# The first SwiGLU half-step rebuilt in Strassen's form, and half of the modulation moved into the attention

## Chip, cores and metric

The kernel runs on one core of one Trainium2 chip. The metric is the device time of one launch in microseconds (us), the median of several runs of the same program. A profile is one further execution, recorded by the hardware profiler; its times are us from its first instruction unless marked ns.

## What is computed

One layer of a diffusion trunk: 512 latent and 128 context tokens (640 in all, the axis `T`), width 1024. Cut to what matters here:

```python
m = adaln(c)                                   # nine modulation vectors m[0..8], silu(c) @ w_ada + b_ada
hh = rmsnorm(x, g[0]) * (1 + m[1]) + m[0]
x = x + 0.5 * m[2] * (silu(hh @ w1) * (hh @ w3)) @ w2     # first half-step, 1024 -> 2816 -> 1024
hh = rmsnorm(x, g[1]) * (1 + m[4]) + m[3]
x = x + m[5] * token_mixer(hh)                            # differential attention (8 heads) and an mLSTM
hh = rmsnorm(x, g[2]) * (1 + m[7]) + m[6]
x = x + 0.5 * m[8] * (silu(hh @ w1b) * (hh @ w3b)) @ w2b  # second half-step
```

The results are the new x, new keys and values, and the final mLSTM states. Everything is float32.

## The kernel before

Features lie on the 128 partitions and tokens along the free axis; `HALF` is 320 tokens, `KT` = 8 tiles of the width, `FB` = 11 blocks of 256 hidden features. A float32 product is made of three matmuls of a rounded type: each operand is split into a high part (rounded by an ACT copy) and a low part (the difference, by one subtraction), and `mm3` adds high x high, high x low and low x high. One such product of a 128 x 128 tile of weights with 320 tokens is three matmuls of 320 columns.

TensorE's instructions stand in the order of the program (`keep_in_program_order`). The other engines' order is set when the program is built, by a planner that simulates durations and prefers, among what is ready, what comes first in the program. DMAs of weights and activations are issued by SP's queue. Weights arrive in two buffers, `raw`, of 1 MB, which all stages share.

**First half-step** (`first_half_step`, L233 on). The blocks `b` run in turn. A block has four up units (f, hf), each with 16 `mm3` on w1 and w3, then `glu` (silu on ACT, the product and the low part `gL` on DVE), and `down` adds the product of the block with w2 to x, tile by tile (16 tiles, 6 matmuls a block each), through `add_residual` on DVE. The weights' high parts are made by ACT and their low parts by POOL (`split_w`, the tiles `wL`, `w3L`). Beside it runs the modulation: `mod_tile` loads 1 MB of `w_ada_c` and makes two columns of it by two DVE products each, which add up along the row (`tensor_tensor_reduce`, with the tile `junk` as output); 28 such tiles give m2 to m8. m0 and m1 come at the very start through TensorE (`Modulate`, the tiles `mrow`, `ps_at`). In the last `down`, the first token half is finished before the second; `to_mixing` collects the squares, and the norm of the mixing for the first half (`norm2(0)`) runs beside the products of the second.

**Mixing.** Groups of the attention's projections come first (`tok_group`, with `norm2_second` inside). Then eight heads, each with five blocks of queries (`qi`): `scores` writes one PSUM tile `sc` that exists once; DVE takes its maximum (`mx`), ACT the exponentials, DVE the weighted difference (`p0`); one block later TensorE transposes it (`turn`, `ps_wT`) and multiplies it with the values (`values`, `ps_o`). In between, `fill.slot()` puts matmuls of other projections, whose weights are again split by ACT and POOL. The heads take from about 620 to 1140 us. Then come the mLSTM and the output projections.

**Second half-step** (from about 1500 us). It has Strassen's form in Winograd's variant: a product of 2 x 2 blocks takes seven block products in place of eight, with sums of the operands. Tokens (two halves) and features (two halves) form the 2 x 2 split; the seven operands are named A11, A12, S2, S1, S3, A22, S4. Block 0 is plain, two units at a time. Then `products` runs over granules: 20 for w1 and w3 of blocks 1 to 10 (`nk` = 4 tiles, 84 matmuls each) and 12 for w2. For each granule, `parts` and `sums` make the split weights and their sums (ACT and DVE alone); `done` receives the four results, adds the shared parts that ACT copied out of PSUM (the tiles `u`), and for w3 writes the gated products into `SO`. `store_g` forms the sums of a finished block in `SO`, makes the high part (ACT) and the low part (DVE) in `g`, and stores both to `g_dram`. For the way down, the blocks are taken in three groups of 4, 4 and 3, and the seven operands of a group come back from `g_dram` into the tiles S and hm:

```python
    GROUPS = ((0, 4), (4, 8), (8, FB))
    ...
    def operand(q, i):
        n = 7 * q + i
        at[q, i] = t = slots[n % 9]
        b0, b1 = GROUPS[q]
        nc.sync.dma_start(out=t[:, :, : b1 - b0].bitcast(F32), in_=g_dram[i, :, :, b0:b1, :])
```

Of the kernel before, what the change touches and what calls it, by code (L numbers as in the profile page):

```python
# [7 lines left out]
F32 = mybir.dt.float32  # L8
# [23 lines left out]
def tile_trunk(ctx: ExitStack, tc: tile.TileContext, a: dict):  # L32
# [52 lines left out]
    x_pool = right.enter_context(tc.tile_pool(name="x1", bufs=1, side="right"))  # L85
    x_all = x_pool.tile([128, KT, T], F32, name="x")
    x = [x_all[:, d, :] for d in range(KT)]
# [50 lines left out]
    def rstd_of(pool, ss, inv_n, shape, tag, bufs=1, ybufs=1):  # L138
        v = pool.tile(shape, F32, tag=tag + "v", name="rv", bufs=bufs)
        y = pool.tile(shape, F32, tag=tag + "y", name="ry", bufs=max(bufs, ybufs))  # L140
        t = pool.tile(shape, F32, tag=tag + "t", name="rt", bufs=bufs)
        ts(v, ss, inv_n, ALU.mult, EPS, ALU.add)
        act(t, v, AF.Ln)
        act(y, t, AF.Exp, scale=-0.5)
        newton_rsqrt(y, v, t)
        return y


    class Stats:


        def __init__(self, x, hf, tmp, eng=pool_e, tag="nsq"):
            self.x, self.hf, self.tmp, self.eng, self.tag = x, hf, tmp, eng, tag
            self.acc = tmp.tile([128, HALF], F32, tag="nacc", name="nacc", bufs=2)

        def add(self, d):
            xs = self.x[d][:, half(self.hf)]
            if d == 0:
                act(self.acc, xs, AF.Square)
                return  # L160
            sq = self.tmp.tile([128, HALF], F32, tag=self.tag, name="nsq", bufs=2)
            self.ins = act(sq, xs, AF.Square).ins  # L162
            if d < KT - 1:
                tt(self.eng, self.acc, self.acc, sq, ALU.add)
# [3 lines left out]
        def rstd(self, psum, ybufs=2):  # L168
# [3 lines left out]
            return rstd_of(self.tmp, ps[:, :HALF], 1.0 / D, [128, HALF], "nr", ybufs=ybufs)  # L172

    def norm_apply(x, n, m_shift, hf, d, rs, hH, hL, tmp):
        c0 = hf * HALF
        shift = m_of(m_shift)
        for s0, s1, j in SEGS[hf]:
            t = tmp.tile([128, HALF], F32, tag="nt", name="nt", bufs=2)
            tv = t[:, : s1 - s0]
            ins = stt(tv, x[d][:, s0:s1], scale[:, n, d, j : j + 1], rs[:, s0 - c0 : s1 - c0], ALU.mult, ALU.mult)  # L180
            sh = shift[:, d, j : j + 1]
            act(hH[:, d, s0:s1], tv, AF.Identity, bias=sh)
            if d % 2 == 0 or n == 0:
                stt(hL[:, d, s0:s1], tv, sh, hH[:, d, s0:s1].bitcast(F32), ALU.add, ALU.subtract)
            else:
                act(tv, tv, AF.Identity, bias=sh)
                tt(pool_e, hL[:, d, s0:s1], tv, hH[:, d, s0:s1].bitcast(F32), ALU.subtract)
        return ins.ins
# [13 lines left out]
    UNITS = [(f, hf) for hf in range(2) for f in range(2)]  # L202
# [3 lines left out]

    def up_group(psum, hh, W, units, g2, tmp, before, tag="g"):

        hH, hL = hh
        ps = [[acc_tile(psum) for _ in range(2)] for _ in units]  # L210
        for k in range(KT):
            before(k)
            for (f, hf), p in zip(units, ps):
                col = k * 256 + f * 128
                cs = half(hf)
                for i in range(2):
                    w = W[i]
                    mm3(p[i], w[0][:, col : col + 128], w[1][:, col : col + 128], hH[:, k, cs], hL[:, k, cs], k == 0, k == KT - 1)
        for (f, hf), p in zip(units, ps):
            glu(g2, f, hf, p, tmp, tag)  # L220

    def glu(g2, f, hf, ps, tmp, tag="g"):
        g = tmp.tile([128, HALF], F32, tag=tag, name="g", bufs=2)
        act(g, ps[0], AF.Silu)
        tt(vec, g, ps[1], g, ALU.mult)
        split_glu(g2, f, hf, g)

    def split_glu(g2, f, hf, g):
        gH, gL = g2
        cs = half(hf)  # L230
        act(gH[:, f, cs], g, AF.Copy)
        tt(vec, gL[:, f, cs], g, gH[:, f, cs].bitcast(F32), ALU.subtract)

    def down(psum, x, gate, blocks, final=None, at_once=1):

# [1532 lines left out]
```

## Time and profile before

| | |
|---|---|
| median of 3 runs | 1930.51 us (1930.28 to 1934.54) |
| the profiled execution | 1934.46 us, span 1932.7 us, mean granted clock 0.982 |
| TensorE busy | 1853.8 us, 96% of the span |
| DVE, ACT, POOL busy | 1280.2, 793.9, 491.5 us |

A matmul record is longer than its share of the engine, because matmuls are pipelined; the pitch is read from a stretch in which TensorE is never idle, by dividing it by the count. A row of the table of stretches gives the stretch, its length, the busy time and count (x) of each engine, the granted clock (1.00 is full), the DMA engines' share and GB/s. A row of groups gives busy time, the mean of one in ns, and the idle time before it with what ended it. In a row of the waits stand the total, the number and the longest.

### The profile page before, as it was taken

What the parts mean: (1) busy time and instruction counts of PE and PEld (TensorE: products, weight loads), DVE (VectorE), ACT (ScalarE), POOL (GpSimd) and SP (SyncE); (2) the same over time, 40 slices, a digit from 0 to 9 for tenths busy, and PEclk for the clock granted to TensorE, in tenths of its full rate; (3) what the DMA queues carried; (4) which work ended last, traced back from release to release, by engine and by line L of the source; (5) the groups of instructions that cost most, each with busy time, mean ns of one, the idle gap of its engine ahead of it and who ended that gap; (6) DMA issues with size and microseconds to landing.
All of it is one profiled execution on the core that took longest, in us unless ns stands there. A gap on an engine that the chain in (4) does not pass through costs nothing. (4 is left out here: it accounts for less than half of the span.)

```text
span 1932.7 us, 31309 instructions
## 1 busy us (share of the span) xinstructions
PE 1853.8 (96%) x12862; PEld 1813.1 (94%) x12862; DVE 1280.2 (66%) x2179; ACT 793.9 (41%) x1374; POOL 491.5 (25%) x183
## 2 busy tenths in 40 slices
PE   5999999999997999999999999999999999999899
PEld 4899999999997999999999998899999999999898
DVE  6898888864556565474575544654146888888776
ACT  4322111222454354454454435566234655554332
POOL 2134322343433223242232222224462000000000
PEclk8999999999998999999999999999999999999999
DMA  8344343442223112122122224445524255557864
GB/s 339 130 169 160 133 172 134 150 153 99 85 84 97 66 65 83 49 92 82 66 83 90 72 85 153 147 139 194 191 97 153 106 183 175 170 183 259 334 243 146
DMA packets 98896, 271.15 MB, mean 140 GB/s; under 512 B 7937, under 2 KB 66817, under 8 KB 81089
## 3 DMA queue, kind: packets, MB, share of 16 engines
q1 hardware_dynamic: 98752, 269.15, 39.7%
q8 instruction: 101, 1.65, 0.3%
q14 instruction: 43, 0.34, 0.1%
HBM read 216.97 MB, written 52.15 MB: 139 GB/s over the span
## 5 line engine op out<-in xcount | busy, mean ns | idle before, releaser
L39 POOL TENSOR_TENSOR wL<-raw,wH 128x2048 fp32r<-128x2048 f32 x67 | 312.3, 4663 | 756.5 <-ACT wH L118 741.7
L52 PE MATMUL ps_p<-hH,wH 128*128 128x320 f32 x864 | 275.2, 319 | 4.9 <-ACT aT L883 2.5
L52 PE MATMUL ps_p<-hH,wL 128*128 128x320 f32 x864 | 268.4, 311 | 0.3 <-POOL wL L39 0.3
L52 PE MATMUL ps_p<-hL,wH 128*128 128x320 f32 x864 | 268.4, 311 | 0.0
L118 ACT ACTIVATE wH<-raw 128x2048 fp32r<-128x2048 f32 x69 | 131.8, 1911 | 213.3 <-PE ps_p L52 75.7
L52 PE MATMUL ps_t<-wH,hH 128*128 128x256 f32 x640 | 187.0, 292 | 1.8 <-DVE x L42 1.8
L52 PE MATMUL ps_t<-wL,hH 128*128 128x256 f32 x640 | 183.3, 286 | 0.3 <-POOL wL L39 0.3
L52 PE MATMUL ps_t<-wH,hL 128*128 128x256 f32 x640 | 183.1, 286 | 0.0
L52 PEld LDWEIGHTS ps_p<-hH,wH 128*128 128x128 f32 x864 | 163.8, 190 | 6.4 <-ACT aT L883 2.8
L52 PEld LDWEIGHTS ps_p<-hL,wH 128*128 128x128 f32 x864 | 164.0, 190 | 0.5
L52 PEld LDWEIGHTS ps_p<-hH,wL 128*128 128x128 f32 x864 | 163.7, 189 | 0.6 <-POOL wL L39 0.6
L52 PE MATMUL ps_f<-S,ww 128*128 128x320 f32 x960 | 152.3, 312 | 7.1 <-DMA S<-g_dram 7.1
L396 DVE CUSTOM_DVE_ANT_0 junk<-raw,csil 128x1024 bf16<-128x1024 f32 x112 | 153.0, 1366 | 8.0 <-DMA raw<-in_w_ada_c 6.9
L52 PEld LDWEIGHTS ps_f<-S,ww 128*128 128x128 f32 x960 | 144.8, 190 | 7.9 <-issue 4.5
L52 PEld LDWEIGHTS ps_t<-wH,hH 128*128 128x128 f32 x640 | 124.7, 195 | 2.2 <-ACT nsq L162 2.0
L52 PEld LDWEIGHTS ps_t<-wL,hH 128*128 128x128 f32 x640 | 124.8, 195 | 0.7 <-POOL wL L39 0.5
L52 PEld LDWEIGHTS ps_t<-wH,hL 128*128 128x128 f32 x640 | 124.8, 195 | 0.0
L52 PE MATMUL ps_f<-hH,wH 128*128 128x320 f32 x384 | 119.6, 315 | 0.0
L832 DVE TENSOR_REDUCE mx<-sc 128x2 f32<-128x1536 f32 (+1 forms) x40 | 59.5, 1488 | 84.6 <-PE sc L52 84.4
L52 PE MATMUL ps_f<-hL,wH 128*128 128x320 f32 x352 | 109.9, 312 | 1.5 <-DVE hL L42 1.4
L52 PE MATMUL ps_f<-hH,w3H 128*128 128x320 f32 x352 | 109.4, 311 | 0.0
L52 PE MATMUL ps_f<-hL,w3H 128*128 128x320 f32 x352 | 109.3, 311 | 0.0
(309 smaller groups left out, 4622.3 us busy)
## 6 DMA issues: line engine op xcount, KB each, us to landing
raw<-in_w_ada_c SPq DMA_DIRECT2D x28, 1024.0 KB, 4.8
g_dram<-g SPq DMA_DIRECT2D x22, 1120.0 KB, 5.4
raw<-in_w2a SPq DMA_DIRECT2D x11, 1024.0 KB, 4.9
raw<-in_w1b SPq DMA_DIRECT2D x11, 1024.0 KB, 5.2
raw<-in_w3b SPq DMA_DIRECT2D x11, 1024.0 KB, 5.3
raw<-in_w1a SPq DMA_DIRECT2D x10, 1024.0 KB, 4.9
raw<-in_w3a SPq DMA_DIRECT2D x10, 1024.0 KB, 4.9
raw_a<-in_w_ada_k SPq DMA_DIRECT2D x8, 1024.0 KB, 9.7
```

What stands on the lines that cost most here:

```text
L39: eng.tensor_tensor(out=out, in0=in0, in1=in1, op=op)
L52: tc.keep_in_program_order(nc.tensor.matmul(*args, **kw))
L118: act(h, raw, AF.Copy)
L396: vec.tensor_tensor_reduce(out=junk, in0=raw[:, i * D : (i + 1) * D], in1=csil[:, v, :], op0=ALU.mult, op1=ALU.add, scale=1.0, scalar=0.0, ...
L832: vec.tensor_reduce(out=mx, in_=sv, axis=AX.X, op=ALU.max)
```

## The change

The classes `Granule` and `HalfStep` are made out of the second half-step's code and used for both. In the first half-step:

- Block 0 stays plain: three units (0,0), (1,0), (0,1) beside the modulation of m0 and m1, then (1,1). The normalised x is written in place of x; `shifts` adds m0 by ACT, `operand_sums` forms S1, S2, S3, S4; x is released and read again from memory before the way down.
- 20 granules up and 12 down follow, with `parts` and `sums` on ACT and DVE. POOL has no subtraction of weights left there.
- The low part of a gated block is not a DVE subtraction (`low_by_dma`): ACT writes minus the high part, and two DMAs of POOL's queue add `SO` to it in place.
- `Columns` makes m2 to m4 (12 tiles of 1 MB, 24 columns' tiles) during granules 0 to 17, two in each of the first six and one in each of the others. m5 to m8 (16 tiles of 1 MB) are made in the attention, two column tiles ahead of each block of queries, in heads 0 to 3.
- Both token halves of x are now finished in the last granule, and `norm2(0)` is called behind it.

For both half-steps the groups on the way down become 3, 4 and 4 blocks, and the last granule's products stand in another order. The squares of a norm are added by DVE (some by POOL before), and the low part of the mixing's normalised input by DVE (every second tile by ACT and POOL before).

```diff
+    GROUPS = ((0, 3), (3, 7), (7, FB))
...
+        def store_g(self, SO, b):
...
+            act(g[:, 0], SO[:, 0:7], AF.Copy)
+            if self.low_by_dma:
+                act(g[:, 1], SO[:, 0:7], AF.Copy, scale=-1.0)
+                for s in (slice(0, 4), slice(4, 7)):
+                    pool_e.dma_start(out=g[:, 1, s], in_=SO[:, s], accum_op=ALU.add)
+            else:
+                tt(vec, g[:, 1], SO[:, 0:7], g[:, 0].bitcast(F32), ALU.subtract)
...
+        units = [(0, 0), (1, 0), (0, 1)]
+        ps = {u: [acc_tile(psum) for _ in range(2)] for u in units}
+        for k in range(KT):
+            start.before(k)
+            for u in units:
+                for i in range(2):
+                    hs.plain(ps[u][i], W[i], *u, k)
+        vec.tensor_copy(identr, ident)
+        hs.begin_gated()
+        for u in units:
+            hs.gate_plain(*u, ps[u])
+        for i in range(2):
+            hs.up[i].load()
+        ps = [acc_tile(psum) for _ in range(2)]
+        for i in range(2):
+            for k in range(KT):
+                hs.plain(ps[i], W[i], 1, 1, k)
+        hs.gate_plain(1, 1, ps)
+        start.shifts()
+        hs.operand_sums(lambda r: x_all[:, 2 * r : 2 * r + 2, :])
+        x_stack.close()
+        hs.store_g(hs.SO, 0)
...
+        def modulation(i):
+            if i < 18:
+                columns.tile()
+                if i < 6:
+                    columns.tile()
+            if i == 18:
+                ada.close()
+                box["x"] = residual()
+                for hf in range(2):
+                    dma(box["x"][1][:, :, half(hf)], a["x"][:, :, half(hf)])
+            if i == 20:
+                natural_log_exp()
...
         def to_mixing(d, hf):
-            if d == 0:
-                stats.append(Stats(x, hf, ntmp))
+            if not stats:
+                stats.extend(Stats(box["l"], h, ntmp) for h in range(2))
             stats[hf].add(d)
-            if d == KT - 1:
-                dma(x_dram[:, :, half(hf)], x_all[:, :, half(hf)])
-            if (d, hf) == (0, 1):
-                natural_log_exp()
-                hh2.extend(hh_tiles(hp))
-                norm2(0)
+            if stats[hf].n == KT:
+                dma(x_dram[:, :, half(hf)], box["x"][1][:, :, half(hf)])
+                if hf == 1:
+                    hh2.extend(hh_tiles(hp))
+                    norm2(0)
...
+    csil = [p.tile([128, D], F32, tag=t, name="csil") for p, t in ((q_pool, "q3"), (k_pool, "k3"))]
+    for v in range(2):
+        nc.sync.dma_start(out=csil[v], in_=csil_dram[v].partition_broadcast(128))
+    rest_of = Columns(csil, k_pool.tile([128, D], BF16, tag="k2", name="junk"), load_raw, range(12, 28))
...
         for qi in range(5):
+            if hd < 4:
+                for _ in range(2):
+                    rest_of.tile()
             if hd or qi:
                 H.scores(qi)
```

The new function of a granule's products, shared by both half-steps, has this order (`tail` are the last two products of the granule before):

```python
into(X, A, gr, A11, True);  p1 = copy_of(X, "nrv")
into(Wb, A, gr, A12, True); done(0, 0, Wb, p1)
tail[0]()                                      # A22 of the granule before, done(0, 1)
work[i + 1][0].sums()
into(X, A, gr, S2, False);  u2 = copy_of(X, ...)
tail[1]()                                      # S4 of the granule before, done(1, 0)
into(Z, A, gr, S1, True);   between(i)         # between is `modulation` in the first half-step
into(X, A, gr, S3, False);  u3 = copy_of(X, "nry"); done(1, 1, Z, u3)
```

745 lines of the change are left out of this document (357 added, 388 removed).

## Prediction

> **What bounds the kernel now.** I read the page first: the busy shares, the forty slices, the chain that ended last.
>
> ```profile
> PE 1853.8 (96%) x12862; PEld 1813.1 (94%) x12862; DVE 1280.2 (66%) x2179; ACT 793.9 (41%) x1374; POOL 491.5 (25%) x183
> PE   5999999999997999999999999999999999999899
> DVE  6898888864556565474575544654146888888776
> POOL 2134322343433223242232222224462000000000
> PE 35%; DVE 3%; DMA 2%; ACT 2%; issue 1%; POOL 0%; SPq 0%; POOLq 0%; ACTq 0%
> ```
>
> TensorE is busy in nearly every slice and is the largest engine of the chain, so matmuls taken out should come out of the time. But the DVE row stands at 8 in the first half-step (slices 1 to 7, counted from 0) and again at 8 in the second (31 to 36): little room under TensorE there. The third view is the table of stretches: first half-step after its start, first three attention heads, start of the second half-step, its up part, the passage to its down part.
>
> ```profile
> 65.00:523.00 458.00, 452.82 (x3055) 451.13 (x3053) 352.83 (x625) 108.51 (x145) 158.37 (x43) 0.99 0.39 138
> 620.00:826.00 206.00, 198.57 (x1525) 193.69 (x1525) 115.85 (x170) 91.84 (x178) 57.50 (x17) 0.98 0.19 65
> 1500.00:1545.00 45.00, 42.41 (x276) 40.24 (x275) 42.48 (x72) 27.11 (x53) 0.00 (x0) 1.00 0.31 109
> 1545.00:1765.00 220.00, 220.00 (x1503) 220.00 (x1502) 185.43 (x237) 114.80 (x152) 0.00 (x0) 1.00 0.52 176
> 1765.00:1820.00 55.00, 47.85 (x294) 47.03 (x293) 40.57 (x58) 21.19 (x25) 0.00 (x0) 0.91 1.00 374
> ```
>
> After the span come PE, PEld, DVE, ACT, POOL, granted clock, DMA share and GB/s. The fourth row is the form that the first half-step is to take: TensorE never idle, 220 us / 1503 = 146.4 ns for a 320-column matmul, DVE at 84%, POOL at nothing.
>
> **Matmuls: -54.5 us.** The first half-step has 11 blocks of 192 up and 96 down matmuls, 3168. In the new form block 0 keeps its 192, each of 20 granules takes 7 x 4 x 3 = 84 (1680), and the down granules 4 x 11 x 21 = 924: 2796. 372 fewer at 146.4 ns.
>
> **Stalls of the old form that go: -8 and -3 us.**
>
> ```profile
> PE ps_y L52 <- DVE g L39: 4.6, 2, 2.3
> PE ps_at L52 <- DVE mrow L356: 3.4, 1, 3.4
> ```
>
> ```profile
> 94.16 4.62 POOL L39 TENSOR_TENSOR wL<-raw,wH 128x2048 fp32r<-128x2048 f32 x1 [34.02 <-ACT wH L118]
> 94.47 4.67 DVE L39 TENSOR_TENSOR gL<-g,gH 128x320 fp32r<-128x320 f32 x1 [1.22 <-ACT gH L231]
> 55.40 4.74 POOL L39 TENSOR_TENSOR w3L<-raw,w3H 128x2048 fp32r<-128x2048 f32 x1 [7.41 <-PE ps_a L52]
> 55.63 4.52 DVE L42 SCALAR_TENSOR_TENSOR scale<-mod,g_norm 128x2 f32<-128x2 f32 x1
> ```
>
> 458 us less 3055 x 0.1464 is 10.8 us that were no matmul time; the statistics matmuls take some of it, and the 4.6 us of waiting with the slower clock behind it some 8. The other rows show why: a DVE operation of 320 columns lasts 4.67 us when a POOL subtraction began 0.3 us before it, and one of 2 columns 4.52 us. In the new form DVE splits the weights and POOL's subtractions go, but for the first block's. The wait of 3.4 us at the start goes with the one at 55 us; I book 3 (0 to 5).
>
> The Trainium skill, "SBUF — State Buffer", section "Who interferes with whom", says that a DVE instruction with two SBUF inputs and a GpSimd instruction that reads SBUF exclude each other for the whole instruction, whichever came first. The trace agrees (4.67 beside 4.62 us). By it alone every such wait of the first half-step would go, and the sum would stand where these rows put it; but it speaks against the other half of the change, which puts such DVE instructions into the attention, where POOL goes on.
>
> **Start of the products: +6 us.** Behind the last group of block 0 TensorE had 96 plain matmuls in the second half-step while DVE made the sums S1, S3, S2; now it has 48.
>
> ```profile
> 1524.82 1.55 DVE L39 TENSOR_TENSOR x<-x 128x640 f32<-128x640 f32 x2
> ...
> 1534.04 0.81 DVE L39 TENSOR_TENSOR S<-x,S 128x640 fp32r<-128x640 f32 x1
> ```
>
> ```profile
> L52 PE MATMUL ps_f<-S,ww x960: 302/309/608, 1537.2 to 1891.6; 128*128 128x320 f32 x192
> ```
>
> The sixth of those splits ended at 1534.85 us and its product began at 1537.2: 2.3 us to spare. 48 matmuls less are 7.0 us, so 4.7 us of idling and something for the clock: 6, with 0 (sums begun earlier) to 10. ACT gets 16 shifts of x more; it is under 65% there (27.11 of 45 us) and hides them.
>
> **DVE in the up part: +12 us.** Its operations, as the second half-step and the old modulation show them:
>
> ```profile
> L39 DVE TENSOR_TENSOR g<-SO,g 128x2240 fp32r<-128x2240 f32 x9 | 22.4, 2493 | 3.5 <-ACT g L1474 3.5
> ```
>
> ```profile
> L396 DVE CUSTOM_DVE_ANT_0 junk<-raw,csil x112: 1206/1218/5524, 67.1 to 418.7; 128x1024 bf16<-128x1024 f32 x112
> L46 DVE TENSOR_SCALAR mod<-mod,b_ada x56: 213/220/4200, 70.9 to 421.6; 128x2 f32<-128x2 f32 x56
> ```
>
> A granule of 84 matmuls takes 12.3 us and DVE 185.43 / 220 x 12.3 = 10.4 us. The low part by DMA removes one 2.49 us operation in two granules: 9.1. A column tile of the modulation costs 2 x 1.218 + 0.22 = 2.66 us. Granules 0 to 5 take two each: 14.4 against 12.3, too much by 2.1 us, 13 in all; granules 6 to 17 take one: 11.8, 96%. Weights are made a granule ahead, which hides some; a stall slows the clock (0.91 in the row of the passage). I take +12, between 0 (the planner sets the columns back into the last granules) and 25. ACT's extra copy (2.07 us in two granules) lies under its 52%. The reload of x goes out on SP behind the last column, and the next granules' weights queue behind it; this is in the range.
>
> **The low part by DMA: +5 us.** No accumulating DMA and no DMA of POOL's queue is in the trace.
>
> ```profile
> 1569.49 2.07 ACT L1474 ACTIVATE g<-SO 128x2240 fp32r<-128x2240 f32 x1
> ...
> 1571.59 2.49 DVE L39 TENSOR_TENSOR g<-SO,g 128x2240 fp32r<-128x2240 f32 x1 [0.17 <-ACT g L1474]
> ...
> 1575.14 0.48 DVE L39 TENSOR_TENSOR SO<-t,s 128x320 f32<-128x320 f32 x1
> ```
>
> ```profile
> g_dram<-g SPq DMA_DIRECT2D x22, 1120.0 KB, 5.4
> ```
>
> SO is read until 1574 us and rewritten at 1575.14. Now a second ACT copy ends at about 1573.6, and two DMAs (655 and 492 KB) read SO after that. With the 5.4 us of the nearest row SO comes free at 1579, 4 us after DVE wants to write it. Behind that write stand, in DVE's order, the weights of the next granule. The lower bound is nothing (the planner puts them in front, as it has them ready), the upper 4 us x 10 blocks = 40, or more where the two DMAs follow one another. I take 0.5 us each, 5, since DVE has other work at hand.
>
> **Passage from up to down: +9 and -3 us.** The fifth row of the table has 55 us for 294 matmuls, which need 43.0: 12 us lost.
>
> ```profile
> PE ps_f L52 <- DMA S<-g_dram: 7.1, 3, 4.2
> ```
>
> That is waiting for seven operands of four blocks, 9.18 MB, 24.5 us at the row's 374 GB/s. The first half-step had no such passage and now gets one; both get groups of 3, 4, 4 blocks, so 6.88 MB, 18.4 us, 6 us less, of which the shorter first granule (63 matmuls, 9.2 us for 12.3) eats 3. So +9 for the first half-step (5 to 14) and -3 for the second (0 to -5). The new order in the last granule I book at nothing: it moves the last evacuation by about 0.5 us.
>
> **Passage to the mixing: +3 us.** The normalisation of the first token half was hidden under the second half's down products. Now both halves end in the last granule.
>
> ```profile
> 525.07 0.36 PE L52 MATMUL ps_t<-wH,hH 128*128 128x256 f32 x1 [1.78 <-DVE x L42]
> ...
> 1506.03 0.48 DVE L48 TENSOR_SCALAR rv<-ps_ss 128x320 f32<-128x320 f32 x1
> ...
> 1510.17 0.48 DVE L42 SCALAR_TENSOR_TENSOR ry<-rt,ry 128x320 f32<-128x320 f32 x1
> ```
>
> From the mean to the finished factor took 4.6 us, and about 1.4 us follow until the first tile: 6 us where 1.78 were idle, less what the other half's last two products (3.5 us) cover. +3, 0 to 6.
>
> **Columns of m5 to m8 in the attention: +15 us.**
>
> ```profile
> L832 DVE TENSOR_REDUCE mx<-sc 128x2 f32<-128x1536 f32 x13 | 22.8, 1757 | 35.8 <-PE sc L52 35.7
> L46 DVE TENSOR_SCALAR nm<-mx 128x2 f32<-128x2 f32 x16 | 20.1, 1259 | 0.2
> ```
>
> ```profile
> PE ps_wT L55 <- DVE p L42: 4.4, 2, 2.6
> PE sc L52 <- ACT p L837: 2.3, 3, 1.3
> ```
>
> 32 column tiles go into 3.2 heads, the 206 us of the second row of the table. At 2.66 us they are 85 us on top of DVE's 115.85: 201 of 206, before any collision with POOL's 57.5 us; the row nm shows what one costs, 1.26 us mean for a 2-column operation. The maximum, the scaling and the weighted difference of each score block queue behind up to four column products (5.3 us), and TensorE's next transposes wait for them; in between it has filling products of some 11 us. Sixteen blocks, half of them late by some 2 us: +15, between 5 and 40. The 16 loads of 1 MB share the two raw buffers with the weights, where the DMA share is 0.19.
>
> **The sum.** -54.5 - 8 - 3 + 6 + 12 + 5 + 9 - 3 + 3 + 15 = -18.5 us. The profiled execution took 1934.46 us (span 1932.7 and 1.8 around it), 3.95 above the median of 1930.51; so 1916.0 by its own time, 1912.0 by the median.
>
> **Rivals.** (1) DVE's extra work is hidden: it keeps 84% in the form of the second half-step without a stall, the planner knows the durations, and the collisions with POOL go. Then the up part, the DMA and 12 us of the attention cost nothing: -18.5 - 12 - 5 - 12 = -47.5, 1883. Against it: 201 of 206 us. (2) The attention becomes DVE's: with collisions its demand passes the 206 us, and the term is 40, not 15: +6.5, 1937; it decides from about 34 us on. For it: the row nm; against it: TensorE waited only some 7 us there. (3) Slower: DVE stands before SO. If its order has the write of SO early and the DMAs land late, each of 10 blocks loses 4 to 8 us of an engine that has none to spare: 40 in place of 5, so +16.5, 1947; it decides from 2.4 us a block. The Trainium skill, "SBUF — State Buffer", section "SBUF: two separate sides", warns that a DMA issued from GpSimd waits for its descriptors while DVE runs an operation that takes both port pairs; no row here shows such a DMA. In this kernel the mechanism would be that the issue waits for DVE operations of up to 2.49 us, which is the upper end of (3). That the change does not compute with fewer matmuls can be excluded from the code.
>
> **Chances.** A measurement of this kernel tells about 0.3%, 5.8 us, from no change. The forecast 0.48, its own range 1896 to 1924, all of it faster. (1) 0.20, faster. (2) 0.15: 0.03 faster, 0.06 same, 0.06 slower. (3) 0.17: 0.02 same, 0.15 slower. So faster 0.71, same 0.08, slower 0.21. The range reaches to 1880 for (1) and to 1945, up to where (3) begins in earnest.
>
> **What would show it.** PE's count falls by 372. A row for the first half-step's up part with 146 ns a matmul shows DVE hidden; under 1503 matmuls in 220 us, with waits of ps_f for DVE's weights, shows the term. Waits of SO for a DMA show (3). In the attention, waits of ps_wT and sc above 7 us show that term, and DVE near its full span there shows (2). POOL falls by some 31 subtractions. I am wrong if TensorE's lost time lies elsewhere, or if the up part is free.

## The result and the profile after

The changed kernel takes 1984.8 us in the median (1980.7 to 1986.1), the kernel before on the same chip 1931.0: a ratio of 1.0271, interval 1.0251 to 1.0291. It is slower by 54 us, where 18.5 us less were forecast. One execution of a later kernel (number 11 below) ran at a granted clock of 0.56 and took 2929 us; it is left out of that kernel's median.

Four marks are set in both traces: the first matmul of the token projections (the end of the first half-step), the first and the last matmul of the scores (the heads), and the first low-part matmul of the second half-step. In traces of different kernels whose heads have the same code, the length of the heads differs by up to 6 us (540.6 to 546.7), so a difference of a few us between two single stretches says little.

| stretch (us) | before | after | difference | forecast |
|---|---|---|---|---|
| start to end of first half-step | 525.1 | 545.4 | +20.3 | -30.5 |
| to the first scores | 99.4 | 100.1 | +0.7 | 0 |
| heads | 511.2 | 546.2 | +35.0 | +15 |
| to the second half-step | 364.6 | 364.1 | -0.5 | 0 |
| second half-step, to the end of the span | 432.4 | 428.5 | -3.9 | -3 |

From the page of the changed kernel, busy times and the slices:

```profile
PE 1822.9 (92%) x12490; PEld 1775.0 (89%) x12490; DVE 1395.3 (70%) x2339; ACT 908.8 (46%) x1527; POOL 349.7 (18%) x150
...
PE   6879888899797878999999998999999999999999
...
DVE  7888887578768888876455553574134988888885
```

The 372 matmuls are gone (12862 - 12490), and TensorE's busy time fell by only 30.9 us (1853.8 to 1822.9), where 54.5 were forecast, while the span grew: its row has 7s and 8s among slices 1 to 15, where it had 9s but for one 7. The same stretches as before the change (first half-step, first heads, start, up part and passage of the second half-step):

```profile
65.00:545.00 480.00, 414.98 (x2688) 408.64 (x2686) 379.38 (x595) 224.76 (x290) 30.79 (x25) 0.94 0.75 243
648.00:854.00 206.00, 174.17 (x1241) 168.83 (x1240) 170.09 (x281) 72.65 (x143) 51.82 (x14) 0.92 0.36 123
1555.00:1600.00 45.00, 42.62 (x272) 41.05 (x271) 41.93 (x72) 25.89 (x50) 0.00 (x0) 0.96 0.30 109
1600.00:1810.00 210.00, 210.00 (x1434) 210.00 (x1433) 179.13 (x230) 109.85 (x147) 0.00 (x0) 1.00 0.53 182
1810.00:1865.00 55.00, 50.43 (x339) 49.47 (x339) 44.30 (x69) 24.59 (x33) 0.00 (x0) 1.00 0.85 307
```

In the first half-step TensorE was idle for 5 us of 458 and is idle for 65 of 480, at a clock of 0.94; the DMA share went from 0.39 to 0.75. In the heads it lost 32 of 206 us, at 0.92, with DVE at 83%. The second half-step's start (272 matmuls in 45 us for 276) and up part (146.4 ns a matmul, as before) are much as they were, and the passage (fifth row) is better: 339 matmuls in 55 us for 294. The waits name what came late:

```profile
PE ps_f L52 <- DVE t L39: 32.3, 5, 11.4
...
PE ps_wT L55 <- DVE p L42: 25.3, 9, 6.4
...
DVE SO L39 <- DMA g<-SO: 24.7, 7, 8.6
...
PE ps_t L52 <- ACT hH L190: 10.9, 1, 10.9
```

The third row is the one the prediction named for its rival (3): DVE waits to write SO until the accumulating DMA has read it. One such place in the order of time (start, duration, engine; idle time in brackets):

```profile
123.16 1.74 POOL L329 DMA_DIRECT2D g<-SO  x2 [31.96 <-ACT g L327]
...
138.26 0.49 DVE L39 TENSOR_TENSOR SO<-t,s 128x320 f32<-128x320 f32 x1 [3.62 <-DMA g<-SO]
...
139.07 2.28 DVE L39 TENSOR_TENSOR ww<-raw,ww 128x2048 fp32r<-128x2048 f32 x1
141.27 1.22 DVE L521 CUSTOM_DVE_ANT_0 junk<-raw_a,csil 128x1024 bf16<-128x1024 f32 x1
...
142.41 0.49 DVE L39 TENSOR_TENSOR t<-ps_f,u 128x320 f32<-128x320 f32 x1
...
142.96 3.57 PE L52 MATMUL ps_f<-hm,wC 128*128 128x320 f32 x12 [10.42 <-DVE t L39]
```

POOL issues the two DMAs at 123.2; SO comes free only at 138.2. Behind the blocked write stand in DVE's order a weight split and a column product of the modulation, and the sum t that frees a PSUM tile comes 4 us later still: TensorE stands for 10.4 us. Four of the five waits for t (21.0 of 32.3 us) follow such a write. The fifth and longest, 11.4 us, follows a column product that had waited 5.4 us for its 1 MB of `w_ada_c`.

### The profile page after: what moved, and what is told of

Read it like the earlier page. It is cut to its first block, busy times and chain, and to the rows that moved or that the text cites. A ratio compares the mean times of both kernels' runs of the same rounds, so it can differ in the third digit from the quotient of the medians.

```text
span 1984.3 us, 30993 instructions
## 1 busy us (share of the span) xinstructions
PE 1822.9 (92%) x12490; PEld 1775.0 (89%) x12490; DVE 1395.3 (70%) x2339; ACT 908.8 (46%) x1527; POOL 349.7 (18%) x150
## 5 line engine op out<-in xcount | busy, mean ns | idle before, releaser
L52 PE MATMUL ps_f<-S,ww 128*128 128x320 f32 x2040 | 327.3, 313 | 19.3 <-DMA S<-g_dram 9.7
L39 POOL TENSOR_TENSOR wL<-raw,wH 128x2048 fp32r<-128x2048 f32 x47 | 218.4, 4648 | 654.9 <-ACT wH L123 640.1
L52 PEld LDWEIGHTS ps_f<-S,ww 128*128 128x128 f32 x2040 | 309.8, 191 | 22.7 <-ACT u L346 11.5
L52 PE MATMUL ps_t<-wH,hH 128*128 128x256 f32 x640 | 189.4, 296 | 10.9 <-ACT hH L190 10.9
L52 PE MATMUL ps_f<-hm,wB 128*128 128x320 f32 x1296 | 199.2, 309 | 0.0
L52 PEld LDWEIGHTS ps_f<-hm,wB 128*128 128x128 f32 x1296 | 192.4, 188 | 0.0
L346 ACT ACTIVATE u<-ps_f 128x320 f32<-128x320 f32 x194 | 83.5, 433 | 232.0 <-PE ps_f L52 229.2
L39 DVE TENSOR_TENSOR raw<-raw 128x512 f32<-128x512 f32 (+3 forms) x192 | 161.4, 843 | 0.7
L39 DVE TENSOR_TENSOR ww<-raw,ww 128x2048 fp32r<-128x2048 f32 (+1 forms) x64 | 142.2, 2221 | 12.4 <-ACT ww L251 12.3
L251 ACT ACTIVATE ww<-raw 128x2048 fp32r<-128x2048 f32 (+1 forms) x64 | 118.8, 1856 | 61.0 <-DVE raw L39 31.3
L52 PEld LDWEIGHTS ps_t<-wH,hH 128*128 128x128 f32 x640 | 127.0, 198 | 11.6 <-ACT hH L190 11.4
L52 PE MATMUL ps_f<-hm,ww 128*128 128x320 f32 x744 | 120.5, 310 | 9.4 <-DVE ww L39 5.1
```

The source lines that it names most:

```text
L39: eng.tensor_tensor(out=out, in0=in0, in1=in1, op=op)
L52: tc.keep_in_program_order(nc.tensor.matmul(*args, **kw))
L251: act(t[0], flat, AF.Copy)
L346: act(t, p, AF.Copy)
```

## Experiments

All times are medians, measured beside the kernel before at 1929 to 1932 us. In the diffs "-" is the changed kernel. The expectations give the theories and their ranges.

**1. Low part by DVE.** Only `low_by_dma` is turned off.

```diff
-        hs.low_by_dma = True
+        hs.low_by_dma = False
```

> The first half-step's low part is made by one DVE subtraction again, as the second makes it; all else as changed. Theory A (the half-step is held by the low part's DMAs: DVE waits before SO, and SP's queue stands before the store of g): 35 to 60 us faster than the changed kernel, 1925 to 1950 us. Theory B (DVE has too much work in the up part): DVE gets 10 x 2.5 = 25 us more, so 10 to 25 us slower, 1995 to 2010. Theory C (the DMA engines are full): 12.6 MB of traffic go, 10 to 15 us faster, 1970 to 1975.

1951.1 us, ratio 1.0105 (1.0080 to 1.0129): 33.8 us come back, a little less than theory A's 35, all of it ahead of the end of the first half-step (545.4 to 510.2); the heads stay at 545. The DMA was the largest single cost of the half-step. A stretch of the up part in the changed kernel and in this one:

```profile
200.00:250.00 50.00, 42.19 (x267) 41.93 (x268) 44.72 (x75) 20.42 (x27) 1.75 (x2) 0.86 0.75 240
```

```profile
200.00:250.00 50.00, 46.20 (x312) 45.41 (x311) 49.99 (x74) 25.13 (x33) 0.00 (x0) 1.00 0.62 219
```

312 matmuls where there were 267, and DVE now has no idle time at all: 49.99 of 50 us. What bounds this stretch without the DMA is DVE.

**2. SO freed early.** The DMA adds the high part, in place of SO, to minus the high part (so the low part is left out); bytes and queue stay, but SO is released as soon as ACT has read it.

```diff
-    pool_e.dma_start(out=g[:, 1, s], in_=SO[:, s], accum_op=ALU.add)
+    pool_e.dma_start(out=g[:, 1, s], in_=g[:, 0, s].bitcast(F32), accum_op=ALU.add)
```

> The two accumulating DMAs read the high part in g in place of SO (the low part becomes zero, so this part of the computation is changed); their number, size and queue stay, only SO is free once ACT has read it. A with DVE's wait before SO as the main path: 25 to 45 us faster, 1940 to 1960. A with the store of g on SP as the main path: under 8 us faster, about 1978. B and C: no change, 1980 to 1988.

1964.8 us, 1.0179 (1.0161 to 1.0197): 20.0 of the 33.8 us, less than the 25 to 45 of the first theory. The rest, 13.7 us, is lost though DVE no longer waits for the DMAs to read SO. What TensorE waits for now is ACT's copies `u` out of PSUM (from 65 to 510 us; first this kernel, then number 1):

```profile
PE ps_f L52 <- ACT u L346: 22.7, 14, 4.9
```

```profile
PE ps_f L52 <- ACT u L346: 2.0, 2, 1.7
```

One of the 14 places, in the order of time:

```profile
260.47 2.06 ACT L325 ACTIVATE g<-SO 128x2240 fp32r<-128x2240 f32 x1
262.43 2.05 ACT L327 ACTIVATE g<-SO 128x2240 fp32r<-128x2240 f32 x1
264.39 0.42 ACT L346 ACTIVATE u<-ps_f 128x320 f32<-128x320 f32 x1
...
264.86 3.53 PE L52 MATMUL ps_f<-S,ww 128*128 128x320 f32 x12 [3.15 <-ACT u L346]
```

The second copy, minus the high part, exists only for the DMA, and `u` stands behind it. In half of the 14 places the two copies stand ahead of `u` without a gap in ACT's work; in six others ACT had waited for a late load of weights. Loads do land later beside the accumulating DMAs: a load of `w1a` takes 7.6 us in the median here, 7.8 in the changed kernel and 5.3 in number 1. This is read from the traces; no run took out the second copy alone.

**3. The same with the store on POOL's queue.** In the changed kernel the store of the low part waits on SP's queue for the DMA (77 us in 11 waits), with the loads of weights behind it.

```diff
-    nc.sync.dma_start(out=self.g_dram[:, :, i, b, :]..., in_=g[:, i].bitcast(F32))
+    q = pool_e if i and self.low_by_dma else nc.sync
+    q.dma_start(out=self.g_dram[:, :, i, b, :]..., in_=g[:, i].bitcast(F32))
```

> As e2_add_high (accumulating DMAs read the high part, so the low part becomes zero), and the store of the low part to memory is issued by POOL's queue, not SP's, so that SP's queue doesn't stand before it with weight loads behind it. If that queue is the rest of the low part's cost (e2 still has 13 us more than e1 in the first half-step): 8 to 13 us under e2's 1964.8, 1952 to 1957. If the DMA engines' time is the rest: no change, 1962 to 1968.

1963.9 us, 1.0180 (1.0158 to 1.0202): no change in the time, so SP's queue is at most a small part of the rest. The traces are less clear than the medians: the first half-step ends at 517.7 us for 523.4 in number 2, and the heads, whose code is the same, take 546.7 us for 540.6.

**4. No columns of m2 to m4 in the first half-step**, the DMA staying (the columns are left out, m2 to m4 zero).

> The columns of m2 to m4 in the first half-step are left out (set to zero). B: DVE loses 24 x 2.66 = 64 us of work, and 50 to 65 us go, 1920 to 1935. A: the DMA's wait stays, and with the other work gone DVE meets it earlier: 10 to 25 us, 1960 to 1975. C: 12 MB of loads go, 15 us, 1970.

1957.2 us, 1.0139 (1.0120 to 1.0158): 27.6 us, a number that none of the three theories had. DVE now has room (33 to 37 of 50 us in the up part) and the DMA still costs as much as before, as number 5 shows. Where DVE waits here, and then what TensorE waits for:

```profile
DVE wB L39 <- ACT wB L236: 56.2, 23, 7.3
DVE SO L39 <- DMA g<-SO: 17.7, 9, 2.8
```

```profile
PE ps_f L52 <- ACT u L346: 18.7, 11, 3.1
```

The first row is DVE waiting for weights whose high part ACT made late, the second the same wait for SO. But TensorE does not wait for the sum t at all in this kernel: its largest wait is for ACT's `u`, as in number 2, and in eight of the 11 places the two copies of SO stand ahead of it without a gap. So the DMA costs the same here by another path.

**5. Neither**: low part by DVE, and the columns of m2 to m4 left out as in number 4.

> As the kernel with the low part by DVE, without the columns of m2 to m4 in the first half-step (those modulation values are zero). Theory (with the low part by DVE the up part is DVE's: 20 granules x 10.4 us + 24 column tiles x 2.66 = 272 us against 20 x 12.3 = 246 of TensorE): without the columns TensorE sets the pace as in the second half-step, the 26 us come back, first half-step ends at 482 to 490 in place of 510, 1951 - 26 = 1925, between 1920 and 1931. Rival (the loss left there is in the passage and the last granule, not in DVE's load): less than 10 us come back, 1941 or more.

1922.5 us, 0.9962 (0.9938 to 0.9986): 28.6 us less than number 1, and the first half-step ends at 483.9. Its up part and the passage:

```profile
250.00:300.00 50.00, 50.00 (x343) 50.00 (x342) 42.26 (x55) 26.59 (x35) 0.00 (x0) 1.00 0.50 172
300.00:350.00 50.00, 46.05 (x299) 45.06 (x298) 39.56 (x61) 22.86 (x31) 0.00 (x0) 0.97 0.85 308
350.00:400.00 50.00, 47.59 (x315) 47.32 (x314) 40.33 (x63) 18.39 (x25) 0.00 (x0) 0.97 0.82 304
```

343 matmuls in 50 us is TensorE without a gap: the form itself does what it does in the second half-step. At that pace 683 matmuls fit into 100 us; the two rows of the passage have 614, so it costs 69 matmuls, 10 us. The four kernels also show that the two costs add: the DMA costs 33.8 us with the columns (1984.8 to 1951.1) and 34.7 without (1957.2 to 1922.5).

**6. No columns in the attention** (left out, m5 to m8 zero).

> The columns of m5 to m8 are left out (set to zero), so the attention has no column products and no loads for them. If they are what makes the heads longer (first to last score block 546 us, 511 before): 32 to 38 us faster, 1947 to 1953, and the heads at 511 us. If the heads are longer for another reason, such as a slower clock carried in from the first half-step: under 10 us.

1949.5 us, 1.0096 (1.0072 to 1.0121): 35.4 us, and the heads take 507.0.

**7. Attention columns cut short**: loads, buffers and the number of instructions stay, the products run over 32 of 1024 elements.

```diff
-    out=self.junk, in0=self.raw[:, self.i * D : (self.i + 1) * D], in1=self.csil[v], ...
+    out=self.junk[:, : self.n], in0=self.raw[:, self.i * D : self.i * D + self.n], in1=self.csil[v][:, : self.n], ...
```

> The changed kernel, with the attention's column products cut to 32 of 1024 elements (that part of the modulation becomes wrong); the 16 loads, the buffers and the count of instructions stay. If DVE's time is what lengthens the heads: as with the columns left out, heads at 507 to 515 us, 1948 to 1955. If the loads and the shared raw buffers do: heads at 535 to 546, 1975 to 1985.

1958.2 us, 1.0146 (1.0123 to 1.0168): 26.6 of the 35.4, between the two ranges. Three quarters of the price goes with the length of the products; the rest stays with the loads, the buffers and the short instructions.

**8. Columns spread**: number 1, with one column ahead of each block of queries over six heads, in two products of 512 each; and the same with `norm2(0)` called one product earlier.

> Low part on DVE as in e1_low_on_dve, and the attention's 32 column tiles spread over 6 heads, one ahead of a block of queries (two ahead of the first two), each product in two halves of 512 because the scratch tile shrinks. The same loads, DVE work 5% more. Theory D (in the attention the column products stand four in a row before the softmax steps, in a stretch that leaves DVE no room): the heads go from 545 to 515-520 us, in all 1919 to 1926. Rival (what counts is the total of DVE work or of loads in the attention, wherever it lies): heads stay at about 545, 1946 to 1955.

> As e5_spread, and the mixing's first norm is called one product earlier, ahead of the last product of the first half-step, since its half of x is finished by then. The wait of the first ps_t for hH (9.9 us in e1) should shrink by 3 to 6 us, and the total with it: 3 to 6 us under e5_spread. If the wait is set by DVE's evacuations and not by the place of the call: the same as e5_spread.

1948.7 and 1949.1 us (1.0093, 1.0076 to 1.0110; 1.0103, 1.0086 to 1.0120), for 1951.1. The heads take 540.4 us in both, for 545.0. That the columns cost so much because they stand close together fell here. So did the guess that the earlier call of the norm gives something back: the wait of the first `ps_t` is 12.3 us with it and 10.0 without. The reason is given below, with the passage to the mixing.

**9. Both costs out**: number 1 without the attention's columns.

> Low part by DVE as in the first experiment, and the attention's columns left out (m5 to m8 are zero). Theory (the two costs are independent): 1951.1 less the 35.4 us that the columns cost = 1916, between 1911 and 1921; the end of the first half-step stays at 510 us and the heads take 507 us. That would be faster than before by 13 to 19 us and would still stand 20 us or more above what the prediction's sum has without these two terms (1912 - 5 - 15 = 1892, less the 12 of DVE's part): the rest is the first half-step's own DVE work. Rival (both are one cost, of columns displaced from one stage into the other): 1925 to 1940.

1915.7 us, 0.9918 (0.9886 to 0.9949), for an expected 1916: the two costs add. That it fits to 0.3 us is chance, since single runs of this kernel lie up to 3.9 us apart.

**10. Columns in the mLSTM and the branch projection** (on number 1), where DVE is busy 168 of 364 us. To make room in SBUF, the tile `num` of the mLSTM has two buffers in place of three, and a scratch tile is of a shorter type; no run has this change alone.

```diff
+            step[0] += 1
+            if step[0] % 2:
+                rest_of.tile()
             m.cell(*st)
...
+            if (mt, hf) != (0, 0):
+                rest_of.tile()
             t = gate_of(gd_dram, g, mt, hf, ...)
```

> Low part by DVE, and the columns of m5 to m8 taken out of the heads and put behind them: one column tile ahead of every second step of the mLSTM and three in each of the four granules of the branch projection behind it. In that stretch of 364 us DVE is busy 168 us. Theory (what counts is what DVE has to do beside them; there it has room for 85 us more): all but 0 to 10 us of the 35 are gone, 1916 to 1926, faster than both kernels; heads 507 to 512 us. Rival (the columns cost TensorE some 1 us each wherever they stand, by their loads and by DVE operations in front of others): 1935 to 1950, the heads short and the mLSTM longer by 20 to 35 us.

1940.4 us, 1.0046 (1.0027 to 1.0065): only 11 of the 35 us come back. The heads are short (506.9), and the stretch behind them is 386.3 us long for 365.8 in number 9. The theory of the idle engine fell, as far as this kernel tests it. Two stretches of it:

```profile
1175.00:1235.00 60.00, 55.79 (x323) 50.48 (x322) 58.42 (x147) 26.80 (x70) 12.37 (x4) 0.97 0.55 188
...
1355.00:1415.00 60.00, 50.74 (x326) 49.82 (x325) 35.96 (x61) 14.07 (x13) 23.57 (x10) 0.91 0.61 228
```

In the first, DVE was filled to 58.42 of 60 us, for 36.60 in number 9: the columns came as soon as their data was there, not evenly. In the second, DVE had room and TensorE had 326 matmuls for 405 in number 9. It waited there for split weights of the branch projection, whose raw data ACT had waited for (1355 to 1415 us):

```profile
PE ps_p L52 <- POOL wL L39: 5.1, 2, 3.7
PE ps_p L52 <- ACT wH L123: 4.2, 1, 4.2
```

```profile
ACT wH L123 <- DMA raw<-in_w_brm: 28.4, 2, 21.0
```

So part of the price here is weights that came late, and not DVE: the 16 loads of the columns share the two `raw` buffers with them.

**11. Groups of 4, 4, 3 on number 10.**

```diff
-    GROUPS = ((0, 3), (3, 7), (7, FB))
+    GROUPS = ((0, 4), (4, 8), (8, FB))
```

> As the kernel with the columns in the mLSTM, but the groups on the way down 4, 4 and 3 blocks as before. Theory (the prediction's step: the passage is set by the operands' bytes, 9.18 for 6.88 MB, 6 us, of which the first granule gives back 3): 2 to 5 us slower in each half-step, together 4 to 10 above that kernel; the wait of ps_f for the operands of the passage grows. Rival (the second half-step's gain of 4.2 us came from the order of the last granule): within 2 us of that kernel.

1944.4 us, 1.0066 (1.0046 to 1.0087): 4.0 us slower, which is the expected sign and the lower end of the size, but the intervals of the two kernels overlap. I count it as pointing that way, no more.

**12. Without POOL's subtractions**, with the columns and without (the low part of the projections' weights is left out in both).

```diff
-        tt(l_eng or pool_e, lo, raw, h.bitcast(F32), ALU.subtract)
+        if l_eng is None:
+            act(lo, raw, AF.Copy, scale=2.0**-13)
+        else:
+            tt(l_eng, lo, raw, h.bitcast(F32), ALU.subtract)
```

> Low part of the gated blocks by DVE, the attention's columns as in the changed kernel, and POOL's subtraction for the low part of the projections' weights replaced by an ACT copy of the same tile (scaled, so that the low part is left out of the products). POOL then has next to nothing in the heads. Theory 'exclusion' (the columns cost TensorE so much because POOL's 4.6 us subtractions and DVE's two-input operations shut each other out, and the columns keep the lock busy): its distance to the next kernel, the same without the columns, is at most 20 us in place of the 35.3 of 1951.1 and 1915.7. Rival 'queue' (the columns stand ahead of the maximum and the difference of the score blocks whatever POOL does): 30 to 36 us.

> The same with the attention's columns left out (m5 to m8 zero): the partner of the kernel before it in this call. Both theories: within 6 us of 1915.7, since POOL's subtractions made TensorE wait for 0.3 us only; ACT has some 8 us a head more. The distance between the two is what is read.

1926.6 us (0.9974, 0.9961 to 0.9987) and 1908.9 us (0.9887, 0.9868 to 0.9905): 17.8 us apart, where 35.3 lie between numbers 1 and 9. Half of the columns' price needs POOL. (The second kernel is 6.8 us faster than number 9, where both theories had at most 6.) What POOL does to DVE, in number 1 (the smallest operation of each score block: ns min/median/max; then the column products in the heads, two to a column tile, with their mean):

```profile
L46 DVE TENSOR_SCALAR nm<-mx x40: 151/160/3814, 619.7 to 1155.0; 128x2 f32<-128x2 f32 x40
```

```profile
L521 DVE CUSTOM_DVE_ANT_0 junk<-raw,csil 128x1024 bf16<-128x1024 f32 x60 | 94.3, 1572 | 10.7 <-DMA raw<-in_w_ada_c 10.5
```

and without POOL's subtractions:

```profile
L46 DVE TENSOR_SCALAR nm<-mx x40: 149/159/170, 605.1 to 1122.7; 128x2 f32<-128x2 f32 x40
```

```profile
L524 DVE CUSTOM_DVE_ANT_0 junk<-raw,csil 128x1024 bf16<-128x1024 f32 x60 | 74.1, 1235 | 19.2 <-DMA raw<-in_w_ada_c 18.9
```

The longest nm falls from 3.81 us to 0.17, the mean column product from 1.57 to 1.24 us. DVE's busy time in the heads is 308 us for 370, with the same work: 62 us of "busy" go when POOL's subtractions go.

**13. Thinned out and split**: on number 1, one column ahead of each block in heads 0 to 3 and 12 in the branch projection.

> Low part by DVE, and the columns of m5 to m8 thinned out and split: one column tile (not two) ahead of each of the 20 blocks of queries of heads 0 to 3, and the other 12 in the branch projection behind the mLSTM. Theory 'density' (a column costs little where DVE has time left around it, and much where the stretch is near full): 8 us for the 20 and 3 for the 12, 1922 to 1932, level with or faster than before. Rival 'a price for each' (1.1 us a column in the heads, 0.75 behind them, as the kernels with all 32 in one place show): 1915.7 + 22 + 9 = 1947, 1942 to 1950.

1957.0 us, 1.0138 (1.0121 to 1.0155), the worst place of all, and above both ranges. With POOL at work a column tile costs 0.8 us (number 10), 1.0 (number 8), 1.1 (number 1) and 1.3 (here), each against number 9. This kernel too has two buffers for `num`.

**14. POOL's subtractions in four pieces**, on number 1.

> Low part of the gated blocks by DVE, columns in the attention as in the changed kernel, and each of POOL's subtractions of 2048 columns cut into four of 512. The work on both engines stays. Theory (a DVE operation that meets POOL waits for the whole POOL instruction, up to 4.6 us): the longest wait falls to about 1.2 us (nm at most 1.4 us in place of 3.8), the heads lose 8 to 18 us of their 35, 1933 to 1943. Rival (the sum of the shut-out time counts, not its pieces): within 4 us of 1951.

1942.7 us, 1.0065 (1.0047 to 1.0083): 8.4 us. The sum came as expected, the place only in part: the heads took 541.0 us for 545.0, where 8 to 18 us less were expected.

```profile
L46 DVE TENSOR_SCALAR nm<-mx x40: 155/166/1251, 614.2 to 1145.9; 128x2 f32<-128x2 f32 x40
```

The longest nm is now 1.25 us, about a quarter of POOL's whole subtraction (4.62 us) in place of 3.81. What a DVE operation loses when it meets POOL goes with the length of POOL's instruction; how much of the 8.4 us this gave is not shown.

**15. Low parts of the weights by DVE**, complete kernels: on number 1, and on the kernel before from the mixing on.

```diff
-        tt(l_eng or pool_e, lo, raw, h.bitcast(F32), ALU.subtract)
+        tt(vec, lo, raw, h.bitcast(F32), ALU.subtract)
```

> The same without pieces, but every low part of the weights made by DVE (2.29 us each, as the two wL of the second half-step show) in place of POOL, 47 of them after the first half-step: nothing is left out. Exclusion theory: DVE's time in the heads stays where it is (some 33 x 2.29 = 76 us more of subtraction, and about 62 us less of waiting: 370 with POOL, 308 without), TensorE loses no more than in the kernel without POOL's work: 1926.6 and up to 12 us, 1926 to 1939, near the kernel before. Rival (DVE's load as such): 1950 or more, since its work has grown by 108 us.

> The kernel before with the same edit from the mixing on (its first half-step keeps POOL's subtractions): tells whether the cure of the kernel above is one of the change's own losses or a gain for both. Exclusion theory: before's heads lose little to it (TensorE's waits there were 12 us in all), so 1924 to 1934, within 0.4% of before; a gain of more than 10 us would say that the kernel before paid for the exclusion too.

The new form with its columns: 1930.7 us, 0.9997 (0.9984 to 1.0011), level with before. The kernel before with the same cure: 1909.4 us, 0.9887 (0.9869 to 0.9904). That is the version that beats both, and it gains 21 us where I expected 10 at most: before's heads fell from 511.2 to 497.0 us and the stretch ahead of them from 99.4 to 91.8. The heads of this kernel, as a stretch and the group of the new subtractions:

```profile
624.00:1130.00 506.00, 500.21 (x3885) 492.82 (x3884) 293.38 (x462) 232.03 (x451) 35.13 (x19) 1.00 0.23 77
```

```profile
L39 DVE TENSOR_TENSOR wL<-raw,wH 128x2048 fp32r<-128x2048 f32 x26 | 59.5, 2288 | 14.5 <-ACT wH L118 14.5
```

DVE does 26 subtractions more, 59.5 us in this window, and has no more busy time than in before's 510 us from 625 on: 293.38 for 295.39. The same subtraction takes POOL 4.62 us. That weights are split sooner is not the gain as far as the waits show it: in the kernel before TensorE waited for `wL` of POOL for 0.6 us in all.

## Why the prediction was wrong, step by step

By the two traces the difference to the forecast is some 70 us: 51 in the first half-step, 20 in the heads, and the rest within 1 us each.

**Matmuls, passage to the way down, second half-step: right.** 372 matmuls went. In number 5, without the two DVE and DMA terms, the first half-step ends 41.2 us earlier than before; the terms for that kernel (-54.5 - 8 - 3 + 6 + 9 + 3) say 47.5. The passage cost 10 us there for a forecast of 9, and the second half-step gained 3.9 us for a forecast of 3. For the start of the products 6 us were booked, and TensorE has no gap from 65 to 120 us in number 5: that term came out near its lower bound. The gains of 8 and 3 us from old stalls were not measured one by one.

**Low part by DMA, +5: the step that failed most.** It cost 33.8 us (number 1), close to the upper bound of 40. Rival (3), with 0.17, had the wait and the size. The step that failed is "I take 0.5 us each, since DVE has other work at hand", and under it the duration: 5.4 us from a plain store to landing. DVE's order had the write of SO ahead of the other work, so that work waited too. The two rows of the changed kernel's DMA view (KB each, median us from issue to landing) and its queue line:

```profile
g<-SO POOLq DMA_DIRECT2D x11, 640.0 KB, 8.3
...
g<-SO POOLq DMA_DIRECT2D x11, 480.0 KB, 11.1
```

```profile
q0 software_dynamic: 3168, 12.62, 3.4%
```

The second lands 11.1 us after its issue, so SO was held some 6 us longer than forecast. Numbers 2 and 3 split the price: 20.0 us go with SO being held, and 13.7 stay with the DMAs when it is not. A second step failed there, one that was put at nothing: "ACT's extra copy (2.07 us in two granules) lies under its 52%". By the traces of numbers 2 and 4 TensorE waits about 20 us for ACT's `u`, in half of the places or more behind that copy, and elsewhere behind weights that landed late. How the 13.7 us divide between the two was not tested. The warning cited from the Trainium skill, "SBUF — State Buffer", section "SBUF: two separate sides", is of a DMA issued from GpSimd that waits for its descriptors while DVE takes both port pairs. Here the 22 DMA instructions lasted 0.85 to 1.2 us each on POOL, and no run shows whether one waited for DVE. Nor was a full DVE needed for the loss, as rival (3) had it: with DVE at 33 to 37 of 50 us the DMA costs 34.7 us.

**DVE in the up part, +12: mis-sized.** The columns there cost 27.6 us in the changed kernel (number 4) and 28.6 without the DMA (number 5 against 1), above the upper end of 25. The forecast had 9.1 us of DVE a granule and summed the excess over the first six granules only (13 us), calling the other twelve, at 96%, free. All together its own figures are 20 x 9.1 and 24 column tiles x 2.66, 246 us of DVE against 246 of TensorE: no room for a wait, and DVE then waited 24.7 us for SO and 11.6 for the columns' loads. How the 27.6 us divide was not tested. Without the DMA a granule has 10.4 us of DVE, which makes 272 us against 246: DVE is over the full time by 26 us, which is near the 28.6 measured, and the row of number 1 shows it at 49.99 of 50 us.

**Passage to the mixing, +3: mis-sized.** TensorE waits 10.9 us for the normalised input where it waited 1.8: 9. The forecast let the other half's last products cover 3.5 us of 6, and they cover nothing. The 6 us themselves were too few, because the chain from the mean (`rv`) to the factor (`ry`) has other work in it. In the changed kernel:

```profile
534.56 0.49 DVE L48 TENSOR_SCALAR rv<-ps_ss 128x320 f32<-128x320 f32 x1 [0.27 <-PE ps_ss L52]
...
536.93 0.47 ACT L149 ACTIVATE ry<-rt 128x320 f32<-128x320 f32 x1
...
538.07 1.80 DVE L973 COPY tab<-g_qn 128x64 f32<-128x64 f32 x1 [3.02 <-DMA g_kn<-in_g_kn]
...
539.79 2.60 DVE L39 TENSOR_TENSOR ropeAq<-tab,g_qn 128x256 f32<-128x256 f32 x1
...
542.65 0.48 DVE L42 SCALAR_TENSOR_TENSOR rt<-ry 128x320 f32<-128x320 f32 x1
```

ACT's part is done at 537.4 and DVE goes on only at 542.65: ahead of it in DVE's order stand tables of the attention (`tab`, `ropeAq`), which wait for a small load and last 1.80 and 2.60 us beside subtractions of POOL. In the kernel before, DVE made these tables later, and `ropeAq` took 0.43 us. Without these 5.25 us, as an estimate from these rows, the wait would have been some 5.7. Number 8's earlier call shows the same: `rv` starts at 495.0 us there, ACT's `ry` is done at 500.1, and DVE goes on at 506.3, behind the same tables. No run took them out.

**Attention columns, +15: mis-sized, and the mechanism half right.** They cost 35.4 us (number 6). The waits were the ones named, but rival (2), which put 40 on them, wanted DVE near its full span, and DVE was busy for 170 of 206 us: its number came near without its condition. TensorE's waits in the heads were 36 us where they had been 12, and its busy time for the same matmuls rose by 10 us as the clock fell (0.91 to 0.98 in the first half of the heads). The forecast had half of the score blocks late by 2 us and nothing for the clock. That the blocks queue behind four column products in a row was not what set the size: spread out, they cost nearly the same (number 8).

What the step left out is POOL. The Trainium skill, "SBUF — State Buffer", section "Who interferes with whom", says that a DVE instruction with two SBUF inputs and a GpSimd instruction that reads SBUF shut each other out for whole instructions. The column products have two such inputs, and the runs agree: their mean fell from 1.57 to 1.24 us when POOL's subtractions went. The operation nm has only one input, so that sentence does not cover it, and yet its longest instance followed the length of POOL's instruction, from 3.81 to 1.25 to 0.17 us. The forecast used the rule for the first half-step's gain, 8 us, and gave the heads no price of their own for it, though the row nm (1.26 us mean for two columns) stood in the prediction. It was worth half of the columns' 35 us, and in the kernel before POOL's subtractions were worth 21 us.

What the runs leave open: the other half of the columns' price. It is there without POOL's subtractions (17.8 us for some 85 us of DVE work), and when DVE makes the low parts itself the heads of the new form with columns take 536.8 us, for 497.0 in the old form without. Queueing on DVE would explain it, and so in part would the loads, which number 10 shows at work; no run took the columns out of the way of the maximum and the difference alone.

## What to carry to other kernels

Before work is moved to an engine "with room", read how much of its busy time is waiting: here a two-column operation that lasted 3.8 us was another engine's instruction. Handing a subtraction to a second engine that shuts the first one out can cost more than doing it oneself; here taking the subtractions behind the first half-step away from POOL, in the old form, was worth 1.1%. And a step that replaces an engine's operation by a DMA must be costed by how long the source stays held and by the operations that prepare it on other engines, not by the time saved: 2.5 us of DVE a block were saved and 3.1 us of the whole lost (33.8 over 11 blocks).

## What the runs showed of the hardware

- A pair of accumulating DMAs of 640 and 480 KB on POOL's queue took 8.3 and 11.1 us to land (medians), where a plain store of 1120 KB took 5.4; POOL was occupied 0.85 to 1.2 us by each issue.
- Stretches of 50 us with TensorE waits of 10 us had a lower granted clock: 0.86 in the changed kernel's stretch with 267 matmuls. Where TensorE has no gap it was 1.00 (number 5, 343 matmuls). In the heads of the changed kernel TensorE's busy time rose from about 500 to 510 us for the same matmuls.
- The longest time of a DVE operation beside POOL followed the length of POOL's instruction (3.81 us with subtractions of 4.62 us, 1.25 with quarters of them, 0.17 without), for an operation of two columns.
